# A hybrid HGRN2 and retention layer on one core: where the rotary tables, the weight sums and the retention's stores are issued

## The chip, the cores and the metric

The kernel runs on one NeuronCore of a Trainium2 chip. A core has five engines with a queue of instructions each, worked off in order: TensorE (PE, matrix products; its weight loads are shown as PEld), VectorE (DVE), ScalarE (ACT), GpSimd (POOL) and SyncE (SP, which only issues DMAs here). Matrix products are written to PSUM banks; everything else lives in SBUF or in HBM. DMAs are issued from the queues of SP, ACT and POOL. The metric is the device time of one execution in microseconds (us); less is better.

## The reference

One layer of a decoder trunk for 1024 tokens of width 1024, all in f32:

```python
u = x * (1.0 + scale1) + shift1
hq, hf, hi, hg, rq, rk, rv, rg, ga, gb = jnp.split(u @ w_in[l], split_at, axis=-1)
ya = _hgrn2(hq, hf, hi, hg, lower_bounds[l]) @ w_pa[l]
yb = _retention(rq, rk, rv, rg, positions) @ w_pb[l]
y = (jax.nn.sigmoid(ga) * ya + jax.nn.sigmoid(gb) * yb) @ w_o[l]
x = _layer_norm(DEEPNORM_ALPHA * x + (1.0 + gate1) * y, ln1_g[l], ln1_b[l])
...
h = jnp.square(jax.nn.relu(u @ w_up[l] + b_up[l]))
y = h @ w_down[l] + b_down[l]
```

HGRN2 is a gated linear recurrence of 8 heads of 128. The retention has 4 heads (queries and keys of 256, values of 512); queries and keys are rotated by `cos` and `sin` of `positions * theta` (the rotary tables), and each head's output of 512 is normalised (mean and variance) before it is gated.

## The kernel before, in words

f32 products are made of three products of rounded halves: each operand is split into a high part (ACT copies it into the rounded type, L184) and a low part (DVE subtracts, L185), and `mm3` (L187) issues high x high, high x low and low x high (L189, L190, L191). Weights come by SP in tiles `raw` (three buffers, L317) and are split into `wh` and `wl`, two tiles ahead of their use.

The stages, in order: `start` (modulated input, L438); the projections of the first pair of HGRN2 heads (`h_dense(0)`); four pairs of HGRN2, where the recurrence of pair p (`h_rec`, many small products, DVE work and masked copies) is woven with the projections of pair p + 1, and the last pair's with the projection of the gate `ga` (`gate_proj`); `r_qk` (queries and keys of the retention, rotated); `r_values`; `r_rec` (the recurrence of the retention); `gates`; `merge`; `out_proj`; `ffn_up`; `ffn_down`.

From `r_qk` on, large products are made by a Strassen-Winograd scheme: 7 products of half-size blocks (q1 to q7) for 8. It needs sums of weight blocks, and sums of the activations.

*Sums of weights.* `block_sums` (L200) lists 224 DMAs from HBM to HBM, 512 KB each, on POOL's queue: four copies and four accumulating copies for each part of a weight matrix, an accumulating one needing what was copied before it. `start_sums(n, pace)` (L223) moves the next n of the list into `prep`; `mm3` takes one from it each time that `pace` columns have been multiplied, and the DMA then waits for that product (`after`, L232). Before the change: 160 from the end of `start` on, one per 9 x 512 columns; 16 in `r_qk`, one per 36 x 512; 32 in `r_rec`, one at each output block there (L1086); 16 in `out_proj`, one per 20 x 512. The projections of the first pair that are left after `start` hold 122,880 columns, those of each later pair 196,608.

*Rotary tables.* `rotary` (L728) makes `cos` and `sin` for 1024 positions in four quarters. In each, DVE reduces the angles in about forty small instructions of 128 x 256 (L764 to L785, `reduce` at L752 to L756), ACT takes two sines, and ACT's queue stores them (L782, L786). Its two tiles are buffers with the tag `gate`; the second and later quarters write the same tiles again, so they wait for the stores. It is a generator: `h_pair_rec` takes a step of it at every third step of the recurrence in the second and third pair (L706), and what is left is done after the third (L1736). `r_qk` loads the tables (L881).

*The order of work.* The program's order is not the order on an engine: a planner goes through the instructions, and where an engine would idle in its own reckoning it draws instructions forward that need nothing more. `after` and `behind` (L793) are edges by hand: the first makes an instruction wait for another's end, the second only fixes their order on a queue.

*The sums of activations in `r_qk`.* `u_sums` (L798, `whole` at L820, `t_sums` at L1150) makes the operands of q5, q6, q7 and q4 on DVE in tiles `rua` and `rub`, which lie where HGRN2's tiles were.

*The retention's recurrence.* `r_main(i)` (L1046) works on half a head, in two blocks of two output tiles; `r_prep(i + 1)` is woven in. An output tile is a bank `po` (three buffers) of 6 to 12 products (L1085). `v_load` (L965) fetches `v` by SP into a `raw` buffer, two blocks ahead; `v_split` splits it. `r_norm` (L1094) takes the statistics on DVE (L1098 to L1100), the power -1/2 on POOL (L1101), the offset on DVE (L1102), and ACT scales the bank into `on` (L1104). Three ticks later (`later` and `tick`, L160; a tick is an output tile) `r_out` (L1107) transposes `on` on PE into the one bank `b` (L1111), ACT copies it to `ot` (L1113, two buffers), and POOL's queue stores it (L1114).

Of the kernel before, what the change touches and what calls it, by code (L numbers as in the profile page):

```python
# [14 lines left out]
ALU = mybir.AluOpType  # L15
# [135 lines left out]
class Trunk:  # L151
# [550 lines left out]

    def h_pair_rec(self, p):
        for hd in (0, 1):
            for n, _ in enumerate(self.h_rec(p, hd)):
                if p in (1, 2) and n % 3 == 1:  # L706
                    next(self.rot, None)
                self.tick()
                yield
        while p == 3 and self.pend:  # L710
            self.tick()
            yield
# [15 lines left out]
    def rotary(self):  # L728
        nc = self.nc
        V = nc.vector  # L730
        MAG = 12582912.0
        TWO_PI = 2.0 * math.pi

        def parts(v, bits):
            out = []
            for b in bits:
                if b is None:
                    out.append(float(np.float32(v)))
                    break
                q = 2.0 ** (math.floor(math.log2(abs(v))) + 1 - b)  # L740
                h = math.floor(v / q) * q
                out.append(h)
                v -= h
            return out

        p2 = parts(TWO_PI, (9, 9, 11, None))
        c16 = math.remainder(65536.0, TWO_PI)
        q16 = parts(abs(c16), (8, 8, None))
        sgn = 1.0 if c16 > 0 else -1.0
        W = 256  # L750

        def reduce(x, n):  # L752
            V.tensor_scalar(n, x, 1.0 / TWO_PI, MAG, op0=ALU.mult, op1=ALU.add)
            V.tensor_scalar(n, n, -MAG, None, op0=ALU.add)
            for c in p2:
                V.scalar_tensor_tensor(x, n, -c, x, op0=ALU.mult, op1=ALU.add)  # L756

        for s in range(T // W):
            cs = slice(s * W, (s + 1) * W)
            two = [self.gp.tile([P, 512], F32, tag="gate", bufs=2, name=self.uid("rot")) for _ in (0, 1)] if s == 0 else two  # L760
            a, m, y, n = (t[:, j * W:(j + 1) * W] for t in two for j in (0, 1))
            pos = self.hp.tile([P, W], I32, tag="pos", bufs=1, name=self.uid("pos"))
            nc.gpsimd.dma_start(pos, self.i["positions"][0:1, cs].to_broadcast([P, W]))
            V.tensor_copy(a, pos)  # L764
            V.tensor_scalar(a, a, self.cst[:, K_THETA:K_THETA + 1], None, op0=ALU.mult)
            V.tensor_scalar(m, a, 1.0 / 65536.0, MAG, op0=ALU.mult, op1=ALU.add)
            V.tensor_scalar(m, m, -MAG, None, op0=ALU.add)
            V.scalar_tensor_tensor(a, m, -65536.0, a, op0=ALU.mult, op1=ALU.add)
            yield
            reduce(a, n)  # L770
            yield
            for c in q16[:2]:
                V.tensor_scalar(y, m, sgn * c, None, op0=ALU.mult)
                reduce(y, n)
                V.tensor_tensor(a, a, y, op=ALU.add)
                yield
            V.scalar_tensor_tensor(a, m, sgn * q16[2], a, op0=ALU.mult, op1=ALU.add)
            reduce(a, n)
            V.tensor_scalar(a, a, 3.1415925, -3.1415925, op0=ALU.min, op1=ALU.max)
            yield  # L780
            nc.scalar.activation(n, a, AF.Sin)
            nc.scalar.dma_start(self.sin_d[:, cs], n)  # L782
            nc.scalar.activation(y, a, AF.Sin, scale=0.5)
            V.tensor_tensor(y, y, y, op=ALU.mult)
            V.tensor_scalar(y, y, -2.0, 1.0, op0=ALU.mult, op1=ALU.add)  # L785
            nc.scalar.dma_start(self.cos_d[:, cs], y)  # L786
            yield
# [177 lines left out]
    def v_load(self, m):  # L965
        if m < 4 * RH:
            t = self.wp.tile([P, 2, 512], F32, tag="raw", bufs=self.raw_bufs, name=self.uid("vr"))
            d = self.nc.sync.dma_start(t, self.v_d[m // 4, m % 4].rearrange("(t p) c -> p t c", p=P))
            if m < 2:
                self.behind(d, self.r_dma)  # L970
            self.r_raw["v", m] = t

# [73 lines left out]
    def r_main(self, i):  # L1046

        nc, mm = self.nc, self.nc.tensor.matmul
        h, hf = divmod(i, 2)
        q, kn, sc = self.r_half.pop(i)  # L1050
        for pr in (0, 1):
            m = 2 * hf + pr
            self.v_load(4 * h + m + 2)
            self.v_split(4 * h + m + 1)
            if 4 * h + m >= 4 * RH - 2:
                self._split_to(self.w_next + 4 * h + m + 3 - 4 * RH)
            vh, vl = self.v_parts.pop(4 * h + m)
            ns = []
            if m == 0:
                self.G = [self.ps("c"), self.ps("c")]  # L1060
            if m < 3:
                kh, kl = kn[pr]
                for e in (0, 1):
                    es = slice(e * P, (e + 1) * P)
                    for c in (0, 1):
                        for j, (l, r) in enumerate(((kh, vh), (kl, vh), (kh, vl))):
                            mm(self.G[e], l[:, c, es], r[:, c], start=m == c == j == 0, stop=c == 1 and j == 2, skip_group_check=m > 0)
                    t = [self.vp.tile([P, 512], F32R, tag=f"vz{m % 2 * 2}{2 * e + c}", bufs=1, name=self.uid("g")) for c in (0, 1)]
                    self.split(*t, self.G[e])
                    ns.append(t)  # L1070
                yield
            sh, sl = sc[pr]
            for c in (0, 1):
                po = self.ps("d")
                pairs = []
                for b, o in ((0, 128 * c), (1, 256))[:c + 1]:
                    os = slice(o, o + P)
                    pairs += [(sh[:, os], vh[:, b]), (sl[:, os], vh[:, b]), (sh[:, os], vl[:, b])]
                cs = slice((2 * pr + c) * P, (2 * pr + c + 1) * P)
                if m > 0:  # L1080
                    for e in (0, 1):
                        gh, gl = self.gs[e]
                        pairs += [(q[0][:, e, cs], gh), (q[1][:, e, cs], gh), (q[0][:, e, cs], gl)]
                for j, (l, r) in enumerate(pairs):
                    x = mm(po, l, r, start=j == 0, stop=j == len(pairs) - 1)  # L1085
                    if j == 0 and self.prep:  # L1086
                        self.after(self.prep.pop(0)(), x)
                self.r_norm(h, 2 * m + c, po)
                self.ada_end()
                self.tick()  # L1090
                yield
            self.gs = ns

    def r_norm(self, h, n, po):  # L1094
        nc, V = self.nc, self.nc.vector
        small = self.rt("small", (P, 16), 4)
        b6, mv, rs, nb = small[:, 0:6], small[:, 6:8], small[:, 8:9], small[:, 9:10]
        V.bn_stats(b6, po)  # L1098
        V.bn_aggr(mv, b6)
        V.tensor_tensor(rs, mv[:, 1:2], self.epso[:, h * 8 + n:h * 8 + n + 1], op=ALU.add)  # L1100
        nc.gpsimd.tensor_tensor(rs, rs, self.mhalf[:, :1], op=ALU.pow)  # L1101
        V.scalar_tensor_tensor(nb, mv[:, 0:1], -1.0, rs, op0=ALU.mult, op1=ALU.mult)  # L1102
        on = self.vp.tile([P, 512], F32, tag=f"vz1{n % 4}", bufs=1, name=self.uid("on"))
        nc.scalar.activation(on, po, AF.Identity, scale=rs, bias=nb)  # L1104
        self.later(3, lambda: self.r_out(h, n, on))

    def r_out(self, h, n, on):  # L1107
        nc = self.nc
# [2 lines left out]
            nc.tensor.transpose(pb[:, e * P:(e + 1) * P], on[:, e * P:(e + 1) * P], self.ident)  # L1111
        ot = self.gp.tile([P, 4, P], F32, tag="gate", bufs=2, name=self.uid("ot"))
        nc.scalar.activation(ot, pb.rearrange("p (e t) -> p e t", e=4), AF.Copy)  # L1113
        nc.gpsimd.dma_start(self.or_d[h].rearrange("(e p) t -> p e t", p=P)[:, :, n * P:(n + 1) * P], ot)  # L1114

    def r_begin(self):
        nc, V = self.nc, self.nc.vector
# [2 lines left out]
        self.r_load(0)  # L1120
        self.v_load(0)
        self.v_load(1)
        self.mask3 = self.rt("mask3", (P, 384), 1)
        causal = self.cst[:, K_CAUSAL:K_CAUSAL + P]
        V.tensor_copy(self.mask3[:, 0:P], causal)
# [532 lines left out]
def build(ctx, tc, ins, out):  # L1658
# [61 lines left out]
    with ExitStack() as s:  # L1720
        k.st = k.pool("start", "right", s)
        k.start()
    k.start_sums(160, 9 * 512)
    k.hst = {}
    with ExitStack() as s:
        k.hp = k.pool("h", "right", s)
        k.hS = [k.hp.tile([P, 4, P], F32, name=f"hS{j}") for j in range(4)]
        for t in k.hS:
            tc.nc.gpsimd.memset(t, 0.0)
        k.rot = k.rotary()  # L1730
        drain(k.h_dense(0))
        for p in range(4):
            nxt = k.h_dense(p + 1) if p < 3 else k.gate_proj("ga", k.ga_d)
            weave(nxt, k.h_pair_rec(p), 16, 36 if p < 3 else 80)
            if p == 2:
                drain(k.rot)  # L1736
    assert not k.prep
    k.start_sums(16, 36 * 512)
    k.r_qk(u12pool.close)
    assert not k.prep  # L1740
    rs = ExitStack()
# [19 lines left out]
    k.u2f = {}  # L1761
    ops = ExitStack()
    k.op = k.pool("op", "right", ops)
    k.start_sums(16, 20 * 512)
    k.out_proj()

    def close():
# [37 lines left out]
```

## Time and profile before

| | |
|---|---|
| median of 3 runs | 2346.02 us (2345.3 to 2348.17) |
| the profiled execution: time, span | 2341.86 us, 2340.1 us |
| granted clock of PE, mean | 0.989 |
| busy: PE, DVE, ACT, POOL | 2249.0, 1574.3, 944.0, 419.4 us |
| DMA: moved, mean rate | 514.27 MB, 220 GB/s |
| of it POOL's queue (q0) and SP's (q1) | 249.08 and 261.82 MB |

The span runs from the first to the last of the program's instructions; the time holds it and what lies around it. The profile names an instruction by its line, its engine, its operation and the tiles that it writes and reads (`wl<-raw,wh`), with shapes. In the lines on waits, "A <- B: t, n, m" says that A waited for B t us in all, in n waits, the longest m. In a timeline, a line holds start and length in us, engine, line, operation, tiles, shapes, and in brackets the idle time of the engine before it and who ended it. A row on stretches holds the stretch, its length, the busy time and count of each engine, the granted clock of PE as a share, the mean busy share of the 16 DMA engines, and GB/s.

### The profile page before, as it was taken

To read this page: it belongs to the slowest core of one execution; us is meant where nothing else is said; L and a number is where in the kernel's file an instruction comes from. 1 tells how busy PE (TensorE), PEld (TensorE's weight loads), DVE (VectorE), ACT (ScalarE), POOL (GpSimd) and SP (SyncE) were. 2 spreads that over 40 slices of the span, in tenths; PEclk is the share of its full clock that TensorE was granted. 3 is DMA by queue.
4 is the path that set the end of the run, shared out by engine and by line. 5 is a ranking of instruction groups with operands and counts; after the bars stand their busy time and mean duration, and the time that the engine had idled before them with its cause. 6 is when DMAs were issued, how large, how long until landed. Compare 5 with 4: busy or idle time off the path is not lost.

```text
span 2340.1 us, 29296 instructions
## 1 busy us (share of the span) xinstructions
PE 2249.0 (96%) x10738; PEld 1869.6 (80%) x10738; DVE 1574.3 (67%) x2715; ACT 944.0 (40%) x1365; POOL 419.4 (18%) x636
## 2 busy tenths in 40 slices
PE   7989999899999998999899999999999999999998
PEld 5878898888888876777778878887877888888886
DVE  8786656567767777666665767666786566544578
ACT  4522222222233332455444444452465556444332
POOL 0323333222112222144331111000200000000000
PEclk9999999999999999999999999999999999999999
DMA  9898989884358767788787688776747565866674
GB/s 271 235 236 219 218 224 205 206 203 108 112 167 232 209 234 269 255 231 245 187 276 246 220 297 272 260 251 209 187 134 264 169 236 195 308 200 196 213 235 154
DMA packets 271936, 514.27 MB, mean 220 GB/s; under 512 B 17600, under 2 KB 143792, under 8 KB 265136
## 3 DMA queue, kind: packets, MB, share of 16 engines
q0 software_dynamic: 73728, 249.08, 38.5%
q1 hardware_dynamic: 196592, 261.82, 34.3%
q8 instruction: 85, 1.39, 0.2%
q10 hardware_dynamic: 1472, 1.50, 0.2%
q14 instruction: 59, 0.48, 0.1%
HBM read 415.85 MB, written 213.92 MB: 269 GB/s over the span
## 4 chain that ended last, share of the span: by engine, by line
PE 46%; DVE 3%; DMA 2%; issue 1%; ACT 1%; POOL 0%; DVEq 0%; SPq 0%; ACTq 0%; POOLq 0%
PE psd L191 8%; PE psd L189 7%; PE psd L190 7%; PE psc L191 4%; PE psc L189 4%; PE psc L190 4%; PE psa L191 3%; PE psa L190 3%; PE psa L189 3%; PE psb L189 1%; PE psb L191 1%; PE psb L190 1%; DMA raw<-in_w_up 1%; DVE wl L185 1%; DMA hr<-hv_d 0%
## 5 line engine op out<-in xcount | busy, mean ns | idle before, releaser
L184 ACT ACTIVATE wh<-raw 128x1024 fp32r<-128x1024 f32 (+1 forms) x296 | 285.9, 971 | 492.2 <-PE psd L190 232.0
L185 DVE TENSOR_TENSOR wl<-raw,wh 128x1024 fp32r<-128x1024 f32 (+1 forms) x296 | 325.9, 1105 | 226.0 <-ACT wh L184 221.3
L189 PE MATMUL psd<-uh,wh 128*128 128x512 f32 x560 | 226.6, 407 | 0.0
L190 PE MATMUL psd<-ul,wh 128*128 128x512 f32 x560 | 225.0, 402 | 0.4 <-DVE ul L185 0.4
L191 PE MATMUL psd<-uh,wl 128*128 128x512 f32 x560 | 223.8, 400 | 0.0
L185 DVE TENSOR_TENSOR hl<-hr,hh 128x1024 fp32r<-128x1024 f32 x96 | 117.0, 1220 | 133.6 <-ACT hh L184 133.4
L184 ACT ACTIVATE hh<-hr 128x1024 fp32r<-128x1024 f32 x96 | 101.3, 1055 | 181.7 <-PE psb L190 69.5
L190 PEld LDWEIGHTS psd<-ul,wh 128*128 128x128 f32 x560 | 106.5, 190 | 20.2 <-DVE ul L185 1.4
L191 PEld LDWEIGHTS psd<-uh,wl 128*128 128x128 f32 x560 | 106.2, 190 | 20.0
L189 PEld LDWEIGHTS psd<-uh,wh 128*128 128x128 f32 x560 | 106.1, 190 | 20.1 <-ACT uh L184 0.7
L646 DVE COPY_PREDICATED hS<-mask,psa 128x128 f32<-128x128 uint8 x288 | 77.1, 313 | 27.6 <-PE psa L639 25.0
L190 PE MATMUL psd<-wl,uh 128*128 128x256 f32 (+1 forms) x304 | 92.2, 303 | 2.0 <-DVE wl L185 2.0
L189 PE MATMUL psd<-wh,uh 128*128 128x256 f32 (+1 forms) x304 | 92.7, 305 | 0.0
L191 PE MATMUL psd<-wh,ul 128*128 128x256 f32 (+1 forms) x304 | 92.1, 303 | 0.0
L639 PE MATMUL psa<-qp,k 128*128 128x192 f32 x384 | 72.6, 329 | 1.3 <-DVE k L615 1.3
L639 PEld LDWEIGHTS psa<-qp,k 128*128 128x128 f32 x384 | 62.1, 189 | 10.3 <-issue 5.7
L1473 POOL TENSOR_TENSOR rs<-rs,mhalf 128x1 f32<-128x1 f32 x16 | 12.6, 789 | 314.2 <-DVE rs L1472 299.2
L189 PE MATMUL psd<-wh,hh 128*128 128x512 f32 x168 | 65.5, 390 | 0.8 <-ACT o L1576 0.8
L190 PE MATMUL psd<-wl,hh 128*128 128x512 f32 x168 | 65.4, 389 | 0.0
L191 PE MATMUL psd<-wh,hl 128*128 128x512 f32 x168 | 65.4, 389 | 0.0
L427 DVE SCALAR_TENSOR_TENSOR adacc<-ar,cond,adacc 128x256 f32<-128x256 f32 x112 | 54.0, 483 | 16.4 <-DMA ar<-in_w_ada 13.5
L190 PEld LDWEIGHTS psd<-wl,uh 128*128 128x128 f32 x304 | 58.0, 191 | 5.1 <-DVE wl L185 3.3
(625 smaller groups left out, 6289.6 us busy)
## 6 DMA issues: line engine op xcount, KB each, us to landing
raw<-in_w_in SPq DMA_DIRECT2D x82, 512.0 KB, 6.8
raw<-in_w_up SPq DMA_DIRECT2D x66, 512.0 KB, 5.8
hr<-hv_d SPq DMA_DIRECT2D x56, 512.0 KB, 3.6
dn_s<-in_w_down POOLq DMA_DIRECT2D x48, 512.0 KB, 6.2
hv_d<-hv POOLq DMA_DIRECT2D x16, 1280.0 KB, 5.7
ar<-in_w_ada POOLq DMA_DIRECT2D x32, 512.0 KB, 4.6
raw<-dn_s SPq DMA_DIRECT2D x32, 512.0 KB, 4.5
hr<-pv_d SPq DMA_DIRECT2D x28, 512.0 KB, 4.6
```

Source lines behind the costliest of these rows:

```text
L184: self.nc.scalar.activation(hi, src, AF.Copy)
L185: self.nc.vector.tensor_tensor(lo, src, hi.bitcast(F32), op=ALU.subtract)
L189: r = mm(out, wh, uh, start=start, stop=False, skip_group_check=more)
L190: mm(out, wh, ul, start=False, stop=False, skip_group_check=more)
L191: l = mm(out, wl, uh, start=False, stop=stop, skip_group_check=more)
L427: self.nc.vector.scalar_tensor_tensor(acc, w, sc, acc, op0=ALU.mult, op1=ALU.add)
L639: nc.tensor.matmul(pa[:, c * 192:(c + 1) * 192].rearrange("p (b w r) -> p b w r", w=2, r=3 * sz), k[:, n * P:(n + 1) * P], mv, start=True, ...
L646: V.copy_predicated(dst, self.mask8[:, o:o + 128].rearrange("p (b two s) -> p b two s", two=2, s=sz), src)
L1473: nc.gpsimd.tensor_tensor(rs, rs, self.mhalf[:, :1], op=ALU.pow)
```

## The change

The rotary tables are made after the last pair of HGRN2 in the program's order, in buffers of the HGRN2 pool with the tag `sg` (the sigmoids of the projections). No weight sums are started before the first pair's projections: 128 begin after them with the same pace, 32 for 16 follow in `r_qk` with half the spacing, the recurrence has 32 as before, and `out_proj` 32 for 16 with 12 x 512 for 20 x 512 columns. In the recurrence a sum no longer waits for a product but stands behind its norm's power on POOL; the norm's offset and scaling are issued two ticks later (`r_scale`), and the output two ticks after that; the stores go to SP's queue; `v` is loaded three blocks ahead.

```diff
     def h_pair_rec(self, p):
         for hd in (0, 1):
-            for n, _ in enumerate(self.h_rec(p, hd)):
-                if p in (1, 2) and n % 3 == 1:
-                    next(self.rot, None)
+            for _ in self.h_rec(p, hd):
                 self.tick()
                 yield
...
-            two = [self.gp.tile([P, 512], F32, tag="gate", bufs=2, name=self.uid("rot")) for _ in (0, 1)] if s == 0 else two
+            two = [self.hp.tile([P, 512], F32, tag="sg", bufs=2, name=self.uid("rot")) for _ in (0, 1)] if s == 0 else two
...
             d = self.nc.sync.dma_start(t, self.v_d[m // 4, m % 4].rearrange("(t p) c -> p t c", p=P))
-            if m < 2:
+            if m < 3:
                 self.behind(d, self.r_dma)
...
-            self.v_load(4 * h + m + 2)
+            self.v_load(4 * h + m + 3)
             self.v_split(4 * h + m + 1)
...
                 for j, (l, r) in enumerate(pairs):
-                    x = mm(po, l, r, start=j == 0, stop=j == len(pairs) - 1)
-                    if j == 0 and self.prep:
-                        self.after(self.prep.pop(0)(), x)
+                    mm(po, l, r, start=j == 0, stop=j == len(pairs) - 1)
                 self.r_norm(h, 2 * m + c, po)
...
         V.tensor_tensor(rs, mv[:, 1:2], self.epso[:, h * 8 + n:h * 8 + n + 1], op=ALU.add)
-        nc.gpsimd.tensor_tensor(rs, rs, self.mhalf[:, :1], op=ALU.pow)
-        V.scalar_tensor_tensor(nb, mv[:, 0:1], -1.0, rs, op0=ALU.mult, op1=ALU.mult)
+        pw = nc.gpsimd.tensor_tensor(rs, rs, self.mhalf[:, :1], op=ALU.pow)
+        if self.prep:
+            self.behind(self.prep.pop(0)(), pw)
+        self.later(2, lambda: self.r_scale(h, n, po, mv, rs, nb))
+
+    def r_scale(self, h, n, po, mv, rs, nb):
+        self.nc.vector.scalar_tensor_tensor(nb, mv[:, 0:1], -1.0, rs, op0=ALU.mult, op1=ALU.mult)
         on = self.vp.tile([P, 512], F32, tag=f"vz1{n % 4}", bufs=1, name=self.uid("on"))
-        nc.scalar.activation(on, po, AF.Identity, scale=rs, bias=nb)
-        self.later(3, lambda: self.r_out(h, n, on))
+        self.nc.scalar.activation(on, po, AF.Identity, scale=rs, bias=nb)
+        self.later(2, lambda: self.r_out(h, n, on))
...
-        nc.gpsimd.dma_start(self.or_d[h].rearrange("(e p) t -> p e t", p=P)[:, :, n * P:(n + 1) * P], ot)
+        nc.sync.dma_start(self.or_d[h].rearrange("(e p) t -> p e t", p=P)[:, :, n * P:(n + 1) * P], ot)
...
         self.v_load(0)
         self.v_load(1)
+        self.v_load(2)
...
-    k.start_sums(160, 9 * 512)
...
-        k.rot = k.rotary()
         drain(k.h_dense(0))
+        k.start_sums(128, 9 * 512)
         for p in range(4):
             nxt = k.h_dense(p + 1) if p < 3 else k.gate_proj("ga", k.ga_d)
             weave(nxt, k.h_pair_rec(p), 16, 36 if p < 3 else 80)
-            if p == 2:
-                drain(k.rot)
+        drain(k.rotary())
     assert not k.prep
-    k.start_sums(16, 36 * 512)
+    k.start_sums(32, 18 * 512)
     k.r_qk(u12pool.close)
...
-    k.start_sums(16, 20 * 512)
+    k.start_sums(32, 12 * 512)
     k.out_proj()
```

## The prediction

> **What bounds the kernel now.** I read the head of the page first, then the busy times of single stages, then who TensorE (PE) waited for in the stages that the change touches, and last the timelines around the longest of those waits.
>
> ```profile
> span 2340.1 us, 29296 instructions
> ...
> PE 2249.0 (96%) x10738; PEld 1869.6 (80%) x10738; DVE 1574.3 (67%) x2715; ACT 944.0 (40%) x1365; POOL 419.4 (18%) x636
> ```
>
> PE is busy 96% of the span: the kernel is bound by PE, and a change can win only what PE stands idle or runs at half clock. The page's average hides where that is, so the next view gives it by stage. Columns: stretch, its length, busy time of PE, PEld, DVE, ACT, POOL with counts, granted clock, DMA share, GB/s. The rows are: the rest of the first projections; the first pair of HGRN2; pairs two and three; the last pair beside the gates `ga`; `r_qk`; the retention's recurrence; its passage into `gates`; `out_proj`.
>
> ```profile
> 60.00:130.00 70.00, 70.00 (x404) 61.75 (x402) 49.13 (x120) 35.85 (x57) 25.51 (x36) 1.00 0.95 246
> 130.00:194.00 64.00, 54.23 (x353) 49.96 (x352) 55.07 (x153) 15.15 (x29) 15.74 (x22) 0.92 0.93 213
> 194.00:505.00 311.00, 299.45 (x1687) 260.13 (x1686) 197.89 (x481) 75.09 (x153) 90.89 (x119) 0.99 0.89 213
> 505.00:655.00 150.00, 146.08 (x752) 121.44 (x751) 111.13 (x234) 44.66 (x84) 29.05 (x41) 1.00 0.47 126
> 655.00:800.00 145.00, 145.00 (x642) 120.09 (x641) 99.09 (x134) 47.44 (x58) 28.06 (x46) 1.00 0.74 209
> 982.00:1140.00 158.00, 145.69 (x797) 118.21 (x795) 105.00 (x233) 91.78 (x138) 67.99 (x99) 0.99 0.85 237
> 1140.00:1185.00 45.00, 35.11 (x141) 27.49 (x140) 32.26 (x34) 18.74 (x26) 11.25 (x18) 0.89 0.51 159
> 1617.00:1715.00 98.00, 97.91 (x453) 81.55 (x454) 75.17 (x113) 40.15 (x73) 19.70 (x30) 0.98 0.68 183
> ```
>
> PE has no gap in the first projections although the DMA engines are 95% busy with the sums there, so taking sums away wins nothing in that row itself. The gaps are in the rows that follow: 64.0 - 54.2 = 9.8 us in the first pair, 12.3 and 9.9 us in the recurrence and its end. The largest wait of each (first row: from 117 to 200; second: from 980 to 1185; us in total, times, longest):
>
> ```profile
> PE psa L603 <- DVE hS L607: 9.8, 1, 9.8
> ...
> PE psb L1111 <- ACT ot L1113: 11.0, 5, 3.8
> ```
>
> **Part 1: sums and rotary leave the start.** The 9.8 us are one wait. DVE's timeline ahead of it (start, length, then in brackets the idle time before and who ended it):
>
> ```profile
> 128.08 0.29 DVE L753 TENSOR_SCALAR rot<-rot 128x256 f32<-128x256 f32 x1 [5.41 <-DMA sin_d<-rot]
> ...
> 138.63 0.71 DVE L606 COPY_PREDICATED hS<-mask,psa 128x256 f32<-128x256 uint8 x1
> ```
>
> So the planner had drawn the rotary work, written into pairs two and three, forward into idle DVE time of the first projections. There each quarter waits until the last quarter's sine and cosine have been stored, the stores stand behind the sums, and DVE, which runs in order, holds the weight splits and the masked copy L606 behind it. PE needs L606's bank. These rows give the rotary's size and place (DVE's and ACT's busy time in two stretches, summed; first and last cosine store; landing of the stores):
>
> ```profile
> sum 140.00, DVE 54.00 ACT 3.12; mean DVE 27.00 ACT 1.56
> L786 ACTq DMA_DIRECT2D cos_d<-rot x4: 326/326/333, 102.5 to 190.1; - x4
> DMA to landing us min/median/max: 4.8/5.6/6.4
> ```
>
> With the rotary gone from here nothing stands ahead of L606 but splits whose data is there. The wait goes, and with it the half clock behind it:
>
> ```profile
> 139.70:143.00 3.30, 2.92 (x8) 2.66 (x9) 2.86 (x8) 0.00 (x0) 0.14 (x1) 0.51 1.17 247
> ```
>
> 3.3 us at clock 0.51 are 1.6 us lost, so up to 9.8 + 1.6 = 11.4 us. What is late next is the copies' own turn (0.71 us each, two banks): I take **10 us won** (8 to 11.4). The sums that left the start win nothing more by themselves. The projections of pairs two to four issue one sum per 9 x 512 columns as before (3 x 196,608 columns, so 128 then and now), and their rows keep about their DMA share.
>
> **Part 2: the rotary beside the last pair.** It needs both `sg` buffers, so it can start when the last sigmoid of pair four has been used (first row, last start 492.9), and it now stands between pair four and `r_qk`, whose first sums (`rub`) take over the memory of its pool. DVE's room until `rub`, and what follows it:
>
> ```profile
> L570 DVE TENSOR_TENSOR q<-psd,sg x4: 681/682/691, 466.5 to 492.9; 128x512 f32<-128x512 f32 x4
> ...
> 494.00:625.00 131.00, 127.08 (x674) 106.02 (x673) 92.81 (x235) 34.02 (x72) 27.77 (x38) 1.00 0.50 123
> ...
> L822 DVE TENSOR_TENSOR rub<-uh,ul x4: 1214/1216/1224, 625.3 to 646.9; 128x1024 f32<-128x1024 f32 x4
> ...
> L185 DVE TENSOR_TENSOR q7l<-rub,q7h x2: 1218/1222/1225, 652.5 to 653.7; 128x1024 fp32r<-128x1024 f32 x2
> L190 PE MATMUL psd<-q7l,wh x12: 389/389/389, 686.8 to 716.1; 128*128 128x512 f32 x12
> ```
>
> DVE idles 131.0 - 92.8 = 38.2 us before `rub`; the rotary needs 54.0. So 15.8 us run after 625.3, and the last cosine must land (5.6): `rub` starts near 646.7, 21 us later than now. The tightest user is q7: made 653.7 + 1.2 - 625.3 = 29.6 us after `rub` starts, read at 686.8; it may start at 657. The cover is 10 us wide. I take **1 us lost** for small delays of the recurrence, which shares DVE with 54 us of foreign work; between 0 and, if the cover fails, the price under the rivals.
>
> **Part 3: the retention's recurrence.** What DVE, ACT and POOL waited for in it, then POOL's timeline at its end:
>
> ```profile
> DVE small L1102 <- POOL small L1101: 29.4, 25, 6.4
> ...
> ACT vh L184 <- DMA vr<-v_d: 12.8, 8, 3.8
> ...
> POOL or_d L1114 <- ACT ot L1113: 47.7, 20, 6.2
> ...
> 1143.41 0.82 POOL L211 DMA_DIRECT2D dn_s<-dn_s  x1 [6.20 <-issue]
> 1144.02 0.82 POOL L1101 TENSOR_TENSOR small<-small,mhalf 128x1 f32<-128x1 f32 x1
> ```
>
> Three things hold the norm's power L1101 on POOL, and DVE waits 29.4 us for it at L1102 with other work behind: the way to POOL and back, 25 times; stores that wait for ACT ahead of it (47.7 us); and sums ahead of it, at 1143.41 one that waited 6.2 us for the sum before it. The change takes each: L1102 is issued after the next norm's statistics, stores go to SP, a sum is issued behind its norm's power. The loads of `v` start one block earlier, 158 / 16 = 9.9 us, against 12.8 us that ACT waited for them in eight waits, none over 3.8. All four lead to the same wait: PE's transposes need ACT's copy L1113 (11.0 us). Those I count as gone. The other 22.2 - 11.0 = 11.2 us of PE's idle time in the two rows wait for DVE, which has 29.4 us fewer to wait but starts the same `gates` work; half of it, 5.6. Sum **17 us won**; ends: 5.5 (half of the 11.0 and nothing else) and 27 (all 22.2 and the 11% of clock in the 45 us row, 5.0).
>
> What the change adds here: SP waits for ACT's copy before each of 32 stores, with the loads of `v`, `k` and `q` queued behind. The nearest row is POOL's: at most 6.2 us in one wait, less than the 9.9 us by which the loads now lead. I take 0.
>
> The Trainium skill (DMA: Bandwidth & Descriptors, "Issuing engines are not separate DMA queues") speaks against the move of the stores: DMAs from any engine share the 16 engines, and another issuer saves only its sequencer's time, "usually small relative to the DMA itself". By it alone the stores win nothing; with a quarter for each of the four causes my 17 would be an estimated 13 and the time 2326. By the trace the price is not the transfer but the 47.7 us that POOL's queue stood at L1114.
>
> **Part 4: sums that come later.** `r_qk` gets 32 sums for 16, one per 18 x 512 columns; `out_proj` 32 for 16, one per 12 x 512. The first projections bear one per 9 x 512 at DMA share 0.95 without a gap of PE: the bound at zero. Pairs two and three, at 0.89, have 311.0 - 299.5 = 11.5 us of gaps, 3.7%, of whatever cause: that bounds the loss by 5.4 us (of 145) and 3.6 (of 98). The shares here (0.74 and 0.68) leave room, so nearer to zero: **1 us lost each**. POOL's powers for `out_proj`'s norms stand behind sums too; with 16 of them PE idles 0.1 us in that row.
>
> **Sum.** 10 + 17 - 1 - 2 = 24 us. The profiled execution took 2341.86 us (span 2340.1), 4.2 us under the median of the runs, 2346.02; I put the difference on the median: 2346.0 - 24 = **2322 us** (by the profiled one, 2318).
>
> **Rivals.**
> *The rotary isn't drawn forward* (slower). It is written behind the last pair; if it runs where it is written, 54.0 us follow 625.3, the last store lands at 684.9, and `rub` starts 27.9 us past the 657 that q7 allows. PE stands 28 us, and the half clock behind it costs the 1.6 us of the first pair: 2322 + 30 = 2352. It decides from a rotary whose last store lands after 657; the gains are used up at 657 + 24 = 681. For it: DVE is 71% busy beside the last pair, and a quarter waits for its stores. Against it: here all four quarters were stored from 190.1 on, while the pairs into which they are written run until 505, and the last pair's DMA share is 0.47 where the first pair had 0.93. Chance 0.10.
> *A weight load comes late in another place.* One such case is there now, in pair three: ACT waited 9.1 us for a load, DVE behind it, and PE at the transposes L698 (longest wait 6.1):
>
> ```profile
> PE psb L698 <- DVE ob L690: 10.7, 6, 6.1
> ...
> 464.62 0.63 ACT L184 ACTIVATE wh<-raw 128x512 fp32r<-128x512 f32 x1 [9.10 <-DMA raw<-in_w_in]
> ```
>
> The pairs keep their sums, and this DMA share makes a second case possible, there or in `r_qk`: 6.1 and the half clock behind it, by the first pair's 1.6, so 8 us: 2330. Chance 0.12; that the present one vanishes as well, 2314, I count in the forecast.
> *SP becomes the queue that blocks.* If a store waits longer than 9.9 us for ACT, `v` comes as late as now and the 17 us go: 2339. Against it stands the 6.2. Chance 0.08.
>
> **How the numbers follow.** Forecast 0.70, rivals 0.10, 0.12, 0.08. The range 2309 to 2341 goes from the upper ends (11.4 + 27 won, 1 lost) to the lower ones (8 + 5.5 won; 5.4 and 3.6 lost) and takes in the second and third rival; the slower rival stays out. A measurement of this kernel can tell about 0.2%, 4.7 us, from no change. Faster by more: forecast, both milder rivals but for a little, 0.86; within: 0.05; slower: 0.09.
>
> **What would show it.** Right: no rotary instruction on DVE before 490 and no wait of L603 near 10 us; PE full from 655 to 800; DVE's wait at L1102 near zero and L1111's under 4 us. Wrong: `rub` starting after 657 with PE waiting for q5 to q7; SP waiting for `ot` with ACT waiting longer for `vr`; a wait in the pairs on a load that now lands over 10 us after its issue.

## The result and the profile after

The kernel after takes 2351.72 us, the median of 20 runs (2344.32 to 2360.15), the kernel before 2345.3, the median of 20 beside it (2339.82 to 2350.18): ratio 1.0027, 95% interval 1.0017 to 1.0037. It is slower by 0.27%, where 24 us of gain were forecast. The profiled execution of after took 2356.89 us, 5 over its median, and that of before 3 under; so of the 15 us between the two traces only 6.4 are the change's, and below a stage is called longer only by waits that have a name or by lengths that several kernels repeat.

The head of the page of after, and its stages in the order of the table in the prediction, each stretch moved to where the same work now lies (columns as there; the rest of `r_qk` is cut to its first 75 us):

```profile
span 2354.9 us, 29281 instructions
...
PE 2258.5 (96%) x10738; PEld 1874.7 (80%) x10738; DVE 1567.7 (67%) x2715; ACT 949.3 (40%) x1369; POOL 392.8 (17%) x604
```

```profile
60.00:130.00 70.00, 70.00 (x403) 61.80 (x404) 24.35 (x42) 27.20 (x47) 3.88 (x7) 1.00 0.23 72
130.00:184.00 54.00, 53.66 (x359) 49.53 (x358) 32.12 (x83) 10.07 (x23) 15.67 (x20) 1.00 0.81 193
184.00:495.00 311.00, 302.46 (x1699) 262.88 (x1698) 201.76 (x496) 74.55 (x155) 93.44 (x121) 0.99 0.90 216
495.00:645.00 150.00, 144.25 (x744) 120.89 (x743) 126.01 (x345) 58.56 (x97) 24.35 (x35) 1.00 0.38 105
645.00:720.00 75.00, 66.81 (x272) 52.96 (x271) 62.87 (x73) 28.06 (x34) 17.70 (x28) 0.93 0.82 239
991.00:1145.00 154.00, 144.19 (x785) 117.02 (x783) 105.29 (x234) 90.18 (x137) 44.44 (x72) 0.99 0.87 235
1145.00:1190.00 45.00, 34.86 (x144) 27.54 (x145) 32.31 (x34) 22.06 (x29) 6.75 (x12) 0.89 0.63 179
1624.00:1737.00 113.00, 108.83 (x502) 89.88 (x503) 81.86 (x122) 43.44 (x77) 32.06 (x48) 0.98 0.91 242
```

What is to be seen: the row of the first pair has lost its hole (53.7 of 54 us busy, clock 1.00). `r_qk`, which had no hole at all, has 8.2 us of them and a clock of 0.93 in its first 75 us. The recurrence and its end, 9.8 and 10.1 us idle, are little better than before. `out_proj`, full before, has 4.2 us idle. The waits behind these rows, after (first pair; `r_qk`; recurrence, five rows; `out_proj`):

```profile
PE psb L698 <- DVE ob L690: 3.5, 1, 3.5
PE psa L603 <- DVE hS L607: 0.3, 1, 0.3
...
PE psd L191 <- DVE wl L185: 3.7, 1, 3.7
...
PE psb L1112 <- ACT ot L1114: 10.8, 5, 4.6
DVE small L1103 <- POOL small L1097: 18.6, 26, 1.2
ACT ot L1114 <- DMA or_d<-ot: 12.0, 6, 3.7
ACT vh L184 <- DMA vr<-v_d: 4.2, 5, 1.5
SPq L1115 <- ACT ot L1114: 68.3, 22, 6.1
...
DVE nm L1533 <- POOL rs L1475: 12.2, 8, 7.1
```

Two rows of before that answer to these and were not shown:

```profile
ACT ot L1113 <- DMA or_d<-ot: 3.4, 4, 1.4
...
DVE nm L1531 <- POOL rs L1473: 8.6, 8, 2.4
```

The first of the waits of after is new. It lies behind the row of the first pair and is the prediction's second rival, a weight load that comes late in another place:

```profile
194.47 0.63 ACT L184 ACTIVATE wh<-raw 128x512 fp32r<-128x512 f32 x1 [6.52 <-DMA raw<-in_w_in]
```

DVE's weight split and PE stood behind it, and PE then ran 5.4 us, from 196.6 to 202.0, at clock 0.50. ACT got its `v` sooner and DVE its powers, as forecast, but PE's wait at the transposes did not move (11.0 and 10.8). ACT's copy now waits 12.0 us for the stores of two copies earlier to land, which I first took for the reason; the runs with more buffers (below) do not bear that out.

**Where `r_qk` lost.** DVE's timeline of after from the end of the rotary on, then PE's at the wait, then two stretches of it:

```profile
641.05 0.43 DVE L782 TENSOR_TENSOR rot<-rot 128x256 f32<-128x256 f32 x1 [4.12 <-ACT rot L781]
641.52 0.29 DVE L783 TENSOR_SCALAR rot<-rot 128x256 f32<-128x256 f32 x1
...
644.50 2.35 DVE L820 TENSOR_TENSOR rub<-uh,ul 128x1024 f32<-128x1024 f32 x2
...
661.72 2.35 DVE L185 TENSOR_TENSOR q6l<-rua,q6h 128x1024 fp32r<-128x1024 f32 x2
663.99 1.28 DVE L1222 TENSOR_TENSOR o<-o,psa 128x512 f32<-128x512 f32 x2
665.18 2.35 DVE L1169 TENSOR_TENSOR rub<-rua,rub 128x1024 f32<-128x1024 f32 x2
667.45 1.22 DVE L185 TENSOR_TENSOR wl<-raw,wh 128x1024 fp32r<-128x1024 f32 x1
```

```profile
664.45 0.61 PE L190 MATMUL psd<-q6l,wh 128*128 128x512 f32 x2
668.72 0.50 PE L191 MATMUL psd<-q6h,wl 128*128 128x512 f32 x1 [3.66 <-DVE wl L185]
```

```profile
664.70:669.80 5.10, 1.44 (x7) 0.89 (x6) 5.10 (x6) 2.57 (x3) 0.00 (x0) 1.00 0.74 118
669.80:676.60 6.80, 6.00 (x15) 4.22 (x14) 6.80 (x9) 0.00 (x0) 0.57 (x1) 0.50 0.51 160
```

`rub` started at 644.5, by the clock close to the 646.7 of the forecast. But the forecast was reckoned in the times of before, and here everything up to `r_qk` comes 9.7 us sooner (the last sigmoid of `ga` at 644.6 for 654.3). Against that sigmoid `rub` is 28.9 us later than in before (0.1 us ahead of it for 29.0), where 21.4 were forecast. PE had taken up q6 by 664.0. DVE was full, 5.10 us of 5.10 and 6.80 of 6.80, with the sums of activations, and a weight split stood in its queue behind them. PE waited 3.66 us, and then ran 6.8 us at clock 0.50, which costs another 3.4; the rest of the 8.2 us are four waits of 2.0 us and less. The Trainium skill (TensorE: Matmul & The Clock Gate, "What's actually happening") has the clock halved after an idle window of about 3.4 us; this wait of 3.66 us agrees, and the 6.8 us are twice that.

**Where `out_proj` lost.** POOL's timeline of after at its end:

```profile
1719.24 0.79 POOL L211 DMA_DIRECT2D dn_s<-dn_s  x1 [0.76 <-issue]
1729.03 0.79 POOL L211 DMA_DIRECT2D dn_s<-dn_s  x1 [9.00 <-issue]
1729.56 0.85 POOL L1475 TENSOR_TENSOR rs<-rs,mhalf 128x1 f32<-128x1 f32 x1
```

A sum stood 9.0 us on POOL's queue, and behind it the power of the last norm, for which DVE waited 7.1 us (2.4 at most before). The view names no releaser of the 9.0 us; the sum before it, issued at 1719.24, took 9.3 us to land, so it ended 0.5 us before the next was issued. Everything after `out_proj` hangs on that norm.

### The profile page after: what moved, and what is told of

The parts are those of the page before. It is cut to its first block, busy times and chain, and to the rows that moved or that the text cites. A ratio compares the mean times of both kernels' runs of the same rounds, so it can differ in the third digit from the quotient of the medians.

```text
span 2354.9 us, 29281 instructions
## 1 busy us (share of the span) xinstructions
PE 2258.5 (96%) x10738; PEld 1874.7 (80%) x10738; DVE 1567.7 (67%) x2715; ACT 949.3 (40%) x1369; POOL 392.8 (17%) x604
```

## The experiments

Theory: the rotary's late end costs `r_qk` what the first pair had won; the doubled sums cost at POOL's queue; the recurrence wins little because of the stores' landing. Rivals: the doubled sums cause all of `r_qk`'s loss; the recurrence only loses its gain to its surroundings. Kernels compared with each other ran on one chip in one sitting with their own runs of before (e1 to e4, e5 to e8, e9 to e12, e13 to e15); across sittings the ratios to before are compared.

| kernel | what it is | median us | ratio to before (95%) |
|---|---|---|---|
| after | all | 2351.72 | 1.0027 (1.0017 to 1.0037) |
| e1_rot_only | rotary moved | 2345.09 | 1.0001 (0.9991 to 1.001) |
| e2_sums_only | sums moved, doubled later | 2348.09 | 1.0008 (0.9993 to 1.0022) |
| e3_recurrence_only | recurrence changed | 2339.99 | 0.9975 (0.9962 to 0.9988) |
| e4_sums160 | sums moved, not doubled | 2332.55 | 0.9947 (0.9933 to 0.9962) |
| e5_sums160_rec | e4 + e3 | 2327.53 | 0.992 (0.9906 to 0.9935) |
| e6_after_sums160 | e5 + e1 | 2345.65 | 0.999 (0.9977 to 1.0002) |
| e7_ot4 | e5, copy back into `on` | 2345.83 | 0.9989 (0.9977 to 1.0) |
| e8_pool_stores | e5, stores on POOL | 2333.38 | 0.9945 (0.9927 to 0.9963) |
| e9_ot_four | e5, four copy buffers | 2326.41 | 0.9916 (0.9901 to 0.993) |
| e10_sp_stores_only | e4 + stores on SP | 2327.86 | 0.9919 (0.9905 to 0.9933) |
| e11_outproj_early | after, `out_proj`'s sums denser | 2363.43 | 1.0073 (1.0056 to 1.0091) |
| e12_after_rot_back | after, rotary back | 2339.43 | 0.9975 (0.9961 to 0.9989) |
| e13_outproj32 | e5, `out_proj` doubled | 2332.96 | 0.9943 (0.9928 to 0.9957) |
| e14_rqk32 | e5, `r_qk` doubled | 2335.91 | 0.9958 (0.9945 to 0.9971) |
| e15_sp_ot_four | e10, four copy buffers | 2332.07 | 0.9941 (0.9929 to 0.9953) |

**One part at a time.** e1 has the diff's four edits of the rotary alone (`h_rec` without `next(self.rot, None)`, tag `sg`, no `k.rot`, `drain(k.rotary())` behind the last pair). e2 has the edits of `start_sums` alone. e3 has the edits of `v_load`, `r_main`, `r_norm`, `r_scale` and `r_out` alone. e4:

```diff
-    k.start_sums(160, 9 * 512)
...
         drain(k.h_dense(0))
+        k.start_sums(160, 9 * 512)
```

> The rotary alone is moved beside the last pair; sums and recurrence are as in the kernel before. Theory (the rotary's late end takes the cover that r_qk's sums had): the 9.8 us wait of L603 goes or shrinks below 4, since the quarters no longer stand ahead of the masked copy, so HGRN2 ends 6 to 10 us earlier; r_qk loses 5 to 9 us of that again in stalls at its first projections (u_sums late), and the time is 2338 to 2346. Rival (r_qk's loss comes from the doubled sums alone): the first pair wins the same, r_qk has no stall over 1 us, and the time is near 2336.

> Only the sums are moved: none beside the first projections, 32 instead of 16 in r_qk and in out_proj. The rotary stays in pairs two and three, as in the kernel before. Theory: without sums the sine stores land early, the 9.8 us wait goes as well (8 to 10 us won), and the doubled sums cost 4 to 6 us in r_qk and 4 to 8 in out_proj: 2343 to 2348. Rival (doubled sums cost nothing, r_qk's loss is the rotary's): near 2336, with r_qk as long as before.

> Only the retention's recurrence is changed: sums behind the powers, stores on SP, v one block earlier, the scale two steps later. Theory (the two ot buffers wait for the stores to land, and the planner draws the norm's reader forward): the recurrence wins 3 to 5 us of the 17 forecast, ACT waits about 12 us for or_d before its copies, and the time is 2340 to 2343. Rival (the recurrence's gain was lost because work arrives there later in the kernel after): 10 us or more won, 2335 or less.

> 160 sums as before, but begun after the first projections, with the rest of the sums left as in the kernel before: 128 fall into the pairs, and what is left over of the 160 into the gates behind them. The rotary stays in pairs two and three. Theory (sums beside the first projections hold the sine stores, and the doubled sums later are what gives the gain back): 8 to 10 us won in the first pair and nothing lost later, 2336. Rival (the wait moves to another load of the pairs): the time is within 4 us of the kernel before.

Measured: 2345.1, 2348.1, 2340.0, 2332.6. The rotary alone wins 6.9 us up to the end of HGRN2 (last sigmoid of `ga` at 647.4 for 654.3) and gives all back in `r_qk` (last product with `q7l` at 795.6 for 795.0), with 16 sums there, by the same wait (PE's, e1):

```profile
PE psd L191 <- DVE wl L185: 3.7, 1, 3.7
```

So the rival for `r_qk` falls. e4 is the surprise in size, 12.4 us (0.53% of 2345): the rotary, left where it was, does no harm once no sums hold its stores (PE's waits of e4 in the first pair):

```profile
PE psb L698 <- DVE ob L690: 3.4, 1, 3.4
PE psa L603 <- DVE hS L607: 0.5, 1, 0.5
```

Either edit alone removes the wait of 9.8 us; both together remove it once. e2 and e4 differ only in where 32 sums stand, and by 1.0008 against 0.9947, some 14 us: far more than my 1 + 1. e3 wins 5.9 us of the 17, a little over the theory's 3 to 5; ACT waited 5.8 us for `or_d`, not the 12 expected.

**Together, and the rotary once more.** e5 is e4 with the recurrence of after; e6 is after with e4's sums; e12 is after with the rotary as before (the four edits of e1 undone).

> The 160 sums begun after the first projections (as in e4_sums160) together with the changed recurrence (as in e3_recurrence_only); the rotary stays in pairs two and three, r_qk and out_proj keep their 16 sums. Theory (the two parts win in different stages and add up): 12.8 and 5.3 us won, 2327. Rival (the recurrence's gain is lost when work reaches it earlier or with other sums beside it): 2332 or more.

> The kernel after, but with 160 sums begun after the first projections, and 16 as before in r_qk and in out_proj. The rotary is beside the last pair, now with 32 sums beside the gates that follow. Theory (doubled sums delay the last norm's power in out_proj by 6 to 7 us, and in r_qk together with the late rotary cost 5): about 12 us faster than the kernel after, 2340; out_proj as long as in the kernel before; the one stall of r_qk that waits for the late u_sums stays, near 4 us and its half clock. Rival (the sums' number does not matter, only the rotary's place): 2348 or more.

> The kernel after, with the rotary back in pairs two and three (drawn forward into the first projections, which now have no sums beside them). Theory (r_qk's loss is the rotary's late end): no stall over 1.5 us in r_qk, which takes about 177 us from the last gate to the first store of v (190 in the kernel after), and 8 to 9 us less than the kernel after: 2343. Rival (the doubled sums alone delay r_qk): r_qk takes 185 or more, 2350.

Measured: 2327.5, 2345.7, 2339.4. e5 adds up and beats both kernels. e6 differs from e5 by the rotary alone, and by 18 us, and lies between what the two sides had expected: with 32 sums beside the gates, DVE's queue stands at the rotary there too (e6, DVE):

```profile
592.40 0.29 DVE L771 TENSOR_SCALAR rot<-rot 128x256 f32<-128x256 f32 x1 [4.18 <-DMA cos_d<-rot]
```

and PE waited for it and for the split in `r_qk` (e6, from 515 to 680):

```profile
PE psd L191 <- DVE wl L185: 5.0, 1, 5.0
PE psa L639 <- DVE hS L646: 3.8, 1, 3.8
```

e12 is 12 us faster than after, more than the 8 to 9 expected. Its `rub` starts at 614.7 and the wait for a split is gone; `r_qk` took 182.3 us by the measure of the expectation, between its 177 and its 185. A smaller wait, on ACT, is left over the 1.5 us that the theory allowed (e12, PE from 640 to 830):

```profile
PE psd L189 <- ACT o L1222: 2.0, 1, 2.0
```

The doubled sums alone do not make it: e2 and e14 have the same 32 sums in `r_qk`, and PE waits for nothing there.

**The doubled sums.** e11 is after with the 32 sums of `out_proj` sooner; e13 and e14 are e5 with one of the two doublings and 144 for 160 sums at the start.

```diff
-    k.start_sums(32, 12 * 512)
+    k.start_sums(32, 9 * 512)
```

> The kernel after, but the 32 sums of out_proj are issued one per 9 x 512 columns instead of 12 x 512, so that they are all out when three quarters of the product are done. Theory (the loss is the last norm's power on POOL, which stands behind a sum that waits for the sum before it): out_proj takes about 80 us as in the kernel before (86.8 in the kernel after), 2345. Rival (32 sums load the DMA engines too much, wherever they are): out_proj stays at 86 or more, 2351.

> As e5_sums160_rec, but out_proj gets 32 sums, one per 12 x 512 columns, as in the kernel after, and 144 instead of 160 start after the first projections; r_qk keeps 16. Theory (the last power stands behind a sum): out_proj takes 86 us instead of 80, DVE waits over 6 us once for the power, 2333 to 2335. Rival (its cost was scatter): within 2 us of e5's 2327.5.

> As e5_sums160_rec, but r_qk gets 32 sums, one per 18 x 512 columns, as in the kernel after, and 144 instead of 160 start after the first projections; out_proj keeps 16. Theory A (doubled sums in r_qk cost only beside a late rotary): 2327 to 2329. Theory B (they delay loads of raw by themselves, as e12's one stall of 2.2 us there says): a stall of ACT's o there again, 2330 to 2333.

Measured: 2363.4, 2333.0, 2335.9. e13 has its 5.4 us where the theory put them: from the first offset `nm` of `out_proj`'s norms to the last it took 86.7 us, 79.9 in e5. Other single profiles agree: 80.0 to 80.4 with 16 sums there (before, e4, e6, e14), 86.1 to 87.3 with 32 (e2, after, e12). DVE's longest wait for a power in e13:

```profile
DVE nm L1535 <- POOL rs L1477: 11.8, 8, 6.7
```

e11 missed on both sides, and shows the mechanism best. I had taken it that sums which end early leave the last power alone. Denser, two of them stood at an earlier sum, 8.1 and 8.4 us, ahead of another tile's power, and the stretch of the norms grew to 92.9 us (e11, POOL, then waits of DVE and PE):

```profile
1703.80 0.78 POOL L211 DMA_DIRECT2D dn_s<-dn_s  x1 [8.07 <-DMA dn_s<-dn_s]
...
1716.13 0.79 POOL L211 DMA_DIRECT2D dn_s<-dn_s  x1 [8.43 <-issue]
1716.68 0.84 POOL L1475 TENSOR_TENSOR rs<-rs,mhalf 128x1 f32<-128x1 f32 x1
```

```profile
DVE nm L1533 <- POOL rs L1475: 17.6, 8, 12.4
...
PE psa L1553 <- ACT z L1534: 12.7, 2, 12.5
```

e14 lost 8.9 us against e5 by the ratios, over both theories, and not in `r_qk`, where its PE is never idle (e14, 177 us):

```profile
639.00:816.00 177.00, 177.00 (x783) 146.56 (x782) 118.76 (x163) 56.59 (x71) 45.49 (x71) 1.00 0.88 251
```

Against e13, of the same sitting, its one profile shows a longer `r_values` (158.7 for 151.8 us from the first store of `v` to the last), which scatters by as much between kernels (below). Where those 8.9 us lie stays open.

**The recurrence.** e8 is e5 with `nc.gpsimd.dma_start` for `nc.sync.dma_start` in `r_out`; e10 is e4 with that one edit the other way. e7 and e9, both on e5, change the buffer of the copy (e15 has e9's edit on e10):

```diff
-        ot = self.gp.tile([P, 4, P], F32, tag="gate", bufs=2, name=self.uid("ot"))
+        ot = on.rearrange("p (e t) -> p e t", e=4)
```

```diff
-        on = self.vp.tile([P, 512], F32, tag=f"vz1{n % 4}", bufs=1, name=self.uid("on"))
+        on = self.vp.tile([P, 512], F32, tag=f"vz1{n % 2}", bufs=1, name=self.uid("on"))
...
-        ot = self.gp.tile([P, 4, P], F32, tag="gate", bufs=2, name=self.uid("ot"))
+        if n % 2:
+            ot = self.vp.tile([P, 512], F32, tag=f"vz1{2 + n // 2 % 2}", bufs=1, name=self.uid("ot")).rearrange("p (e t) -> p e t", e=4)
+        else:
+            ot = self.gp.tile([P, 4, P], F32, tag="gate", bufs=2, name=self.uid("ot"))
```

> As e5_sums160_rec, but ACT's copy of the transposes goes back into the normalized tile it came from (four buffers in turn) and is stored from there, so that it no longer waits for a store of two norms earlier to land. Theory (the recurrence's gain is held by the two buffers of ot): no wait of ACT for or_d, PE's wait at the transposes falls from about 10 us to 4, and the time is 4 to 8 us under e5. Rival (PE waits there for the norm's whole chain, whatever the buffers): within 2 us of e5.

> As e5_sums160_rec, but the recurrence's stores are issued from POOL again. Theory of the prediction (the stores' wait for ACT holds the powers behind them): POOL waits some 48 us at the stores again, DVE's wait for the power grows back from 19 to 25 us or more, and the time is 3 to 5 us over e5. Rival (the store's landing is what counts, and the issuer changes nothing): within 1.5 us of e5.

> As e5_sums160_rec, but ACT's copies go to four buffers in turn (the two of ot and two that the normalized tiles gave up, which now take turns in two). Theory (the landing of the stores holds the two buffers of ot, and e7_ot4 only moved that wait to the scaling, because there one buffer had to serve from the scaling to the landing): ACT waits under 3 us for or_d in the recurrence (13.1 in e5), PE at the transposes for under 5 (8.9), and the time is 3 to 6 us under e5's 2327.5. Rival (PE waits for the norm's chain through DVE, POOL and ACT): PE still waits 8 us or more there, time within 2 us of e5.

> As e4_sums160, and of the recurrence's changes the stores on SP alone; the sums stay tied to the matmuls, v is loaded two blocks ahead, the scale follows the norm. Theory A (of the four causes the prediction counted only the stores' queue was real, as e8_pool_stores, which has the other three, equals e4_sums160): 2327 to 2329. Theory B (the stores can leave POOL only because v comes earlier; otherwise SP blocks the loads, the prediction's third rival): 2333 or more, with ACT waiting over 15 us for vr.

> As e10_sp_stores_only, but with four buffers in turn for ACT's copies, as in e9_ot_four. Theory (the landing of the stores costs 3 to 6 us in the recurrence whatever stands around it): ACT waits under 4 us for or_d, 2322 to 2325. Rival (the wait moves to the end of the norm's chain, as in e9): 2326 to 2329.

Measured: 2345.8, 2333.4, 2326.4, 2327.9, 2332.1. First the issuer. e8, with all but the move to SP, is as good as e4 (0.9945 and 0.9947); e10, with that move alone, as good as e5 (0.9919 and 0.992). So of my four causes the stores' queue is worth some 6 us, and the other three together nothing that can be told; the intervals of e8 and e5 overlap a little, those of e4 and e10 touch. e10's one profile does not show the stage itself shorter, so the place of the gain is not shown there. The waits at POOL's queue and the stores' landing from POOL (e8), then the landing from SP (e5):

```profile
POOL or_d L1117 <- ACT ot L1116: 60.6, 21, 7.7
...
DVE small L1105 <- POOL small L1099: 29.3, 24, 3.8
...
DMA to landing us min/median/max: 2.7/5.7/8.7
```

```profile
DMA to landing us min/median/max: 2.3/5.7/9.4
```

The transfer is the same, 5.7 us. By that the rule that I quoted from the Trainium skill (DMA: Bandwidth & Descriptors, "Issuing engines are not separate DMA queues") agrees: the issuer doesn't speed up the transfer. But the move won the 6 us all the same. In e8 POOL's queue stood 60.6 us at the stores, and DVE waited 29.3 us for the powers behind them, 18.4 in e5: that fits the prediction's cause. In e10 against e4 DVE's wait hardly moved (26.1 and 28.1), so there the way by which the 6 us come is not shown.

Then the landing. My theory of the two buffers falls, as far as the time goes. e7 only moved the wait: ACT's scaling waits for the landing (28.6 us, 6.5 at most) and 18 us are lost. With four buffers the wait is nearly gone in e9, and gone from the copies in e15, but no time is won. ACT and PE in e9, then in e15:

```profile
PE psb L1114 <- ACT ot L1119: 5.1, 2, 3.5
...
ACT ot L1119 <- DMA or_d<-ot: 3.9, 1, 3.9
```

```profile
PE psb L1111 <- ACT ot L1116: 10.4, 5, 3.4
...
ACT on L1104 <- DVE small L1102: 36.5, 25, 5.5
```

e9 comes near the lines that the theory asked for (ACT under 3 us, PE under 5) and is 1.1 us under e5, less than can be told. e15 is 5 us over e10 by the ratios, above both its expectations, with ACT waiting for the norm (36.5 us; 26.0 in e10) and PE as long as ever. The rival has the time of e9 right, but not PE's wait there (5.1 us, where it asked for 8). That the norm's own chain through DVE, POOL and ACT stands behind the buffers is what e15's 36.5 us suggest; no run changes that chain alone.

## Why the prediction was wrong, point by point

By ratios times 2345: moving the sums wins 12.4 us (e4) and the recurrence 6 (e3, e5 against e4). The doubled sums cost 14 (e2 against e4), the rotary 12 (after against e12). That is 8 lost; measured 6.4. The prices depend on their surroundings: the doubled sums cost 13 without the late rotary (e12 against e5) and 9 with it (after against e6), the rotary 16 without the doubled sums (e6 against e5, 18 by their medians).

- **Part 1 (10 won): the mechanism right, the size partly luck.** The wait of 9.8 us is 0.3 and the clock behind it 1.00. Stores behind sums holding the rotary, and the rotary holding DVE, is what e1, e2 and e4 each undo. But the 9.7 us at the end of HGRN2 are a sum of more: the first head ended 8.3 us sooner than in before, the fourth only 4.9 (9.3 in e1, which has no late weight load near 194), and the fifth 11.2, as pair three's wait of 6.1 us is gone. So the second rival's late load (chance 0.12) came up in the first pair, while the one in the third was gone. The prediction also named two edits that each remove the wait, and I didn't ask what the second is worth then: nothing, and it has a price.
- **Part 2 (1 lost): wrong, the step "The cover is 10 us wide".** Cost: 12 us by the medians. From the last sigmoid of `ga` to the last product with `q7l` it took 140.7 us in before, 142.9 in e12 and 152.3 in after. Two things were wrong in the step. First, the rotary was to fill all of DVE's idle time and to shift `rub` by 21.4 us; it shifted it by 28.9, for DVE still idled 13.2 of the 131.6 us from 484.0 to 615.6 (the forecast's stretch, some 10 us sooner), and 11.6 of the 29.4 behind them, 8.2 of these for the rotary's own sines on ACT. That `rub` lay within 2.2 us of 646.7 by the clock is luck: Part 1's gain, which was not counted there, hid the error. Second, the cover was counted to one operand, q7, as if DVE's queue held nothing else that PE needs. PE came to q6 first, 19.9 us after the last sigmoid for 27.1 in before, and what it waited for was no operand but a split of weights in DVE's queue behind the sums of activations, which fill DVE, but for 1.2 us, from 644.5 to the split at 667.45. The split I had not priced. My slower rival had the rotary as its cause but the wrong point of decision: in the times of before `rub` came at 654.2 (644.5 + 9.7), within its 657, and PE stood all the same.
- **Part 3 (17 won): the wait was the wrong one.** "All four lead to the same wait", PE's at the transposes, "those I count as gone": it stayed (11.0, 10.8). Shorter waits ahead of it, DVE's for the power (29.4 to 18.6) and ACT's for `v` (12.2 to 4.2 from the recurrence's start to 1165), did not shorten it; why is not shown. 6 us came, as far as the medians can tell all from the stores' issuer. The 5.6 from DVE's freed time did not come. The rival of SP as a blocking queue didn't come true, not even in e10, with `v` no earlier: ACT waited 6.6 us for it.
- **Part 4 (1 + 1 lost): a size, off by 12 us.** In `out_proj` I wrote that POOL's powers stand behind sums and went on by DMA shares and PE's idle time with 16 sums. What counts is how close an accumulating sum follows the one that it needs: POOL then stands for its landing with a power behind it. 5.4 us by e13. The other 8.9 (e14) are measured, not located.

## What to carry to other kernels

Count a cover from the consumer's own arrival, not by the clock of the old trace: an edit upstream moves both ends. Filler work does not fill all idle time of an engine; and a cover holds only if the queue that feeds the consumer has room, not only the operand. When two edits remove the same wait, price the second without its gain. An in-order queue that issues DMAs with dependences is no place for small operations that others wait for; the cheap cure is to move the DMA, as long as the other queue has slack.

## What the runs showed of the hardware

The clock was halved after a shorter wait than 3.4 us, too, but not after each. After PE's wait of 2.01 us for ACT's `o`, which ended at 712.73 in after, the first of these stretches follows; the second is what follows a wait of 3.19 us at the transposes, which ended at 1118.40:

```profile
714.10:717.60 3.50, 2.95 (x8) 1.76 (x6) 1.97 (x4) 0.90 (x1) 1.41 (x3) 0.51 1.05 398
...
1118.40:1123.00 4.60, 4.60 (x29) 4.09 (x29) 3.67 (x11) 2.65 (x5) 1.97 (x4) 1.00 0.61 166
```

So a wait of 2 us can cost nearly as much again, and the length of a wait alone does not tell whether it will; here the measurement differs from the page named above.

A stage that no edit touches, `r_values`, took from 151.5 us (e1) to 160.9 (e6) with DVE's instructions in the same order. The times to landing of its 32 loads `ar`, added up from the trace, go along: 152.3 us in e1, 152.9 in before (153.6 us), 160.7 in after (158.6), 169.9 in e6. Each load takes 4 to 8 us, DVE waits for it with a weight split behind, and PE for that. So a difference of 5 us between two single profiles is no finding by itself, and the medians of whole kernels had to carry the verdicts.
